# Modulation in two halves of the channels, with the first 256 tokens' products between them, at the start of a hybrid decoder block

## The chip, the cores and the metric

The kernel runs on one core of a Trainium2 chip. The time is the device time of one execution in microseconds (us). Engines: TensorE (PE in the rows; PEld its weight loads), VectorE (DVE), ScalarE (ACT), GpSimd (POOL) and SyncE (SP, which only issues transfers here). An engine works through its own instructions in their order; a semaphore lets it wait for another engine or for a transfer (DMA).

## The reference, cut to what matters

One decoder block on 2048 tokens of 1024 channels. The change touches the modulation, the normed input h and the first products with `w_in`:

```python
mod = jax.nn.silu(c) @ w_ada + b_ada            # c: (1, 1024), w_ada: (1024, 3072)
shift, scale, gate = jnp.split(mod, 3, axis=-1)
h = rms_norm(x, norm_w) * (1.0 + scale) + shift
z = h @ w_in                                     # w_in: (1024, 10240)
a, b, g_conv, q, k, v, g_attn, m_conv, m_attn = jnp.split(z, SPLIT_POINTS, axis=-1)
...
q = rope(rms_norm(q, q_norm_w), positions)       # angles = positions * inv_freq
k = rope(rms_norm(k, k_norm_w), positions)
```

Behind it come 12 attention heads of three dilations, a convolution branch, gates and the output projection, none of which the change touches.

## The kernel before

**Units and steps.** The projections of q, k and v are made head by head; one head is a unit, and unit 0 is the first. A unit has 16 steps, one for each block of 128 tokens. A step is 24 products on TensorE (line 373): for each of the eight channel blocks k the upper part of h by the upper part of the weights, the upper by the lower, and the lower by the upper (`hT_hi`, `hT_lo`, `wh_u`, `wl_u`), all added up in one bank of PSUM, `pz`. Then ScalarE squares q and k (`sq`, line 390) and copies v (`qkv`, line 400), GpSimd takes the inverse roots, and VectorE scales q and k out of the bank (`qk`, line 404) and turns them by the angles (lines 411 to 414). The banks `pz` alternate between two. A step of unit 0 also carries the preparation of the token blocks to come: a hook between two of the 24 products.

**h.** x comes in blocks of 128 tokens as rows. ScalarE squares each half (line 261), GpSimd makes the inverse root of the mean in three small operations (lines 264, 114, 115), ScalarE scales the block in two halves (line 269). TensorE turns tiles of 128 x 128 by products with `ident` (line 279, `pt_x`; four tiles a call, two channel blocks of two token blocks). Then the modulation is put on: for the first two token blocks by `h_first` (the upper part by ScalarE straight from PSUM, line 285; the same in full by VectorE, line 290; the lower part is the difference, line 292; the full one is stored to `h_d`), for later ones by `h_part` (lines 302 to 307). `hf` is its buffer, of which there are two; a buffer comes free when its store to `h_d` has ended.

**Modulation.** `c`, `b_ada` and `norm_w` are loaded as rows into `nat` and turned at once by TensorE (`pt_c`, line 147) into `cols`. silu(c) is `sc`. `w_ada` comes in eight row blocks, each in two loads of 1024 columns (shift, scale). Row blocks 1, 3 and 5 are weighted by `sc` and added up on VectorE (`sums`, lines 192 and 194); the other five and the sum go through TensorE (`ada_row`, line 201) into four banks of one row each. ScalarE copies the four rows out (`row`, line 221), 16 small turns make columns of them (`pt_ada`, line 224), and two operations of VectorE make `mod` (lines 225, 226).

**Angles.** The positions are loaded element by element into a column form (`pos_i`, line 141), the frequencies are spread over the partitions (`freq`, line 142), and VectorE makes the reduced angles in `tab` (128 x 1024) in 15 operations, between which the sums of `w_ada` stand. ScalarE takes the sines (lines 212, 213).

**What sets the order.** The order of TensorE is the program's from the units on, with x1's and x0's turns behind the modulation's fourth row block; elsewhere a scheduler places what is not pinned (`keep` pins an instruction to its place in the program). SP issues the transfers, except x0 to x3 and the first three raw weights (`raw_u`, line 343), which ScalarE's queue issues. ScalarE splits each raw weight into `wh_u` (line 349) and another engine into `wl_u` (line 352).

**Hooks of unit 0.** In step j the tiles of a later pair of token blocks are turned and modulated, two calls in an even step and two in an odd one, before product 11 and before product 19; x is squared and scaled at products 4, 9 and 12.

Of the kernel before, what the change touches and what calls it, by code (L numbers as in the profile page):

```python
# [10 lines left out]
F32 = mybir.dt.float32  # L11
# [43 lines left out]
def tile_hybrid_block(  # L55
# [67 lines left out]
    with pool("start", side="right") as st:  # L123
        keep = tc.keep_in_program_order
        nat = st.tile([4 * KC, P], F32, name="nat")
        cols = st.tile([P, 4 * KC], F32, name="cols")
        keep(nc.sync.dma_start(nat[:KC, :], c.rearrange("b (k p) -> (b k) p", p=P)))
        keep(nc.sync.dma_start(nat[KC : 3 * KC, :], b_ada[: 2 * D].rearrange("(k p) -> k p", p=P)))
        keep(nc.sync.dma_start(nat[3 * KC :, :], norm_w.rearrange("(k p) -> k p", p=P)))
        pos_i = st.tile([P, NB], I32, name="pos_i")  # L130
        freq = st.tile([P, 64], F32, name="freq")
        was = {}

        def ada_load(k):
            for half in range(2):
                wa = was[k, half] = st.tile([P, D], F32, tag="wa", name=f"wada{k}_{half}", bufs=10)
                last = keep(nc.sync.dma_start(wa, w_ada[P * k : P * k + P, D * half : D * half + D]))
            return last

        ada_load(0)  # L140
        keep(nc.sync.dma_start(pos_i, positions.rearrange("b (j p) -> p (b j)", p=P)))
        keep(nc.sync.dma_start(freq, inv_freq[None, :].to_broadcast([P, 64])))
        for k in range(1, KC):
            last_ada = ada_load(k)

        pt = bank("t", "pt_c")
        nc.tensor.transpose(pt[:, : 4 * KC], nat, ident[: 4 * KC, : 4 * KC])
        keep(nc.vector.tensor_copy(cols, pt[:, : 4 * KC]))
        th = consts.tile([P, KC], F32, name="th_c")
        with tc.high_priority():  # L150
            nc.scalar.activation(th, cols[:, :KC], AF.Tanh, scale=0.5)
        keep(nc.vector.scalar_tensor_tensor(sc, th, 1.0, cols[:, :KC], op0=ALU.add, op1=ALU.mult))
        keep(nc.vector.tensor_scalar(sc, sc, 0.5, None, op0=ALU.mult))

        pos_f = st.tile([P, NB], F32, name="pos_f")
        keep(nc.vector.tensor_copy(pos_f, pos_i))
        a = tab[:, :, 0, :]
        n = tab[:, :, 1, :]
        na = st.tile([P, NB, 64], F32, name="na")

        def angles():

            v = nc.vector

            yield v.tensor_tensor(a, pos_f[:, :, None].to_broadcast([P, NB, 64]),
                                  freq[:, None, :].to_broadcast([P, NB, 64]), op=ALU.mult)
            yield v.tensor_scalar(n, a, 1.0 / (2 * math.pi), MAGIC, op0=ALU.mult, op1=ALU.add)
            yield v.tensor_scalar(n, n, -MAGIC, None, op0=ALU.add)
            yield v.tensor_scalar(na, n, MAGIC * 2048, None, op0=ALU.add)
            yield v.tensor_scalar(na, na, -MAGIC * 2048, None, op0=ALU.add)  # L170
            yield v.tensor_sub(n, n, na)
            for part in TWO_PI:
                for t in (na, n):
                    yield v.scalar_tensor_tensor(a, t, -part, a, op0=ALU.mult, op1=ALU.add)
            yield v.tensor_scalar(a, a, -PI_LO, PI_LO, op0=ALU.max, op1=ALU.min)

        turning = angles()

        def angle_steps(count):
            for _, ins in zip(range(count), turning):  # L180
                keep(ins)


        BY_SUM = (1, 3, 5)
        acc = [bank("z", "ada0"), bank("z", "ada1"), bank("s", "ada2"), bank("s", "ada3")]
        sums = st.tile([P, 2 * D], F32, name="sums")

        def ada_sum(k):
            for half in range(2):
                part, wa = sums[:, D * half : D * half + D], was.pop((k, half))  # L190
                if k == BY_SUM[0]:
                    keep(nc.vector.tensor_scalar(part, wa, sc[:, k : k + 1], None, op0=ALU.mult))
                else:
                    keep(nc.vector.scalar_tensor_tensor(part, wa, sc[:, k : k + 1], part, op0=ALU.mult, op1=ALU.add))

        def ada_row(k):
            for half in range(2):
                wa = sums[:, D * half : D * half + D] if k is None else was.pop((k, half))
                col = ones[:, :1] if k is None else sc[:, k : k + 1]
                for i in range(2):  # L200
                    last_row = nc.tensor.matmul(acc[2 * half + i][:1, :], col, wa[:, 512 * i : 512 * i + 512],
                                                start=(k == 0), stop=(k == KC - 1))
            return last_row

        angle_steps(3)
        ada_sum(1)
        angle_steps(4)
        ada_sum(3)
        angle_steps(3)
        ada_sum(5)  # L210
# [1367 lines left out]
```

## Time and profile before

| what | us |
|---|---|
| median of three runs | 2396.71 |
| lowest, highest | 2389.79, 2397.10 |
| the profiled execution, its time | 2388.53 |
| its span, first to last instruction | 2386.7 |
| mean granted clock of TensorE | 0.996 |

A row of the timeline reads: start, length, engine, line of the kernel, operation, output <- inputs, shapes and types, number of instructions put together, and in brackets how long the engine was idle before and what ended that. Lengths of one TensorE row overlap, since products are pipelined: the distance of two starts is the pitch. In a window row the first figure is its length, then come the busy time of TensorE, its weight loads, VectorE, ScalarE and GpSimd, the granted clock of TensorE (1.00 is full speed), the share of time in which the 16 transfer engines were busy, and GB/s. A row of waits has the waiting engine and tile, what released it, the total wait, how many, and the longest.

### The profile page before, as it was taken

Reading aid. Unit: us, or ns where it says so; the run is one execution under the profiler, and the core shown is the slowest. Engines: PE = TensorE matmul, PEld = TensorE weight load, DVE = VectorE, ACT = ScalarE, POOL = GpSimd, SP = SyncE. Lnnn points to the kernel's source line nnn. Section 1 sums busy time; section 2 is a strip of 40 time slices with the busy share of each in tenths; the row PEclk is TensorE's granted clock in tenths of the full one; section 3 lists DMA queues with packets and bytes.
Section 4 is the critical chain, followed back from the end, with each engine's and each line's share of the span. In section 5 each row is a group of like instructions: output and inputs, shape, how many; then the busy total and the mean of one; then the engine's idle time right before and its main releaser. Section 6 shows DMA issues by size and latency. Waiting matters only on the chain.

```text
span 2386.7 us, 38725 instructions
## 1 busy us (share of the span) xinstructions
PE 2343.6 (98%) x12353; PEld 2088.3 (87%) x12353; DVE 1737.6 (73%) x4091; ACT 1024.4 (43%) x2850; POOL 843.8 (35%) x1003
## 2 busy tenths in 40 slices
PE   6999999999999999999999999999999999999999
PEld 2989999999999999998888888788888888878887
DVE  5865655555555777777699999979977778887654
ACT  4833433333444554456444444644444444333221
POOL 4421111111111111112577778755556730000221
PEclk9999999999999999999999999999999999999999
DMA  7633544544552222225545445744443569876552
GB/s 260 219 119 109 162 123 143 156 149 155 161 164 81 66 80 59 60 84 163 174 141 165 162 159 194 232 129 152 150 150 124 173 193 333 287 256 205 186 168 102
DMA packets 354106, 378.56 MB, mean 159 GB/s; under 512 B 29737, under 2 KB 251209, under 8 KB 353903
## 3 DMA queue, kind: packets, MB, share of 16 engines
q1 hardware_dynamic: 316414, 316.64, 42.1%
q10 hardware_dynamic: 37488, 59.46, 7.2%
q8 instruction: 98, 1.61, 0.3%
q14 instruction: 106, 0.86, 0.1%
HBM read 235.34 MB, written 140.64 MB: 158 GB/s over the span
## 4 chain that ended last, share of the span: by engine, by line
PE 89%; DVE 3%; DMA 3%; ACT 2%; POOL 1%; issue 1%; SPq 0%; ACTq 0%; DVEq 0%; POOLq 0%
PE pz L373 31%; PE paab L899 7%; PE yc L1207 5%; PE pcab L899 4%; PE pag_mc_d L899 4%; PE oa L1489 4%; PE pag_g_d L899 3%; PE ya L1207 3%; PE pag_ma_d L899 3%; PE po L502 3%; PE ps L453 3%; PE pcg_g_d L899 2%; PE oc L1489 2%; PE pbab L899 2%; PE paag L899 2%; PE pcg_mc_d L899 2%
## 5 line engine op out<-in xcount | busy, mean ns | idle before, releaser
L373 PE MATMUL pz<-wh_u,hT_lo 128*128 128x384 f32 x1536 | 537.6, 350 | 5.3 <-DVE hT_lo L292 3.8
L373 PE MATMUL pz<-wh_u,hT_hi 128*128 128x384 f32 x1536 | 518.9, 338 | 4.2 <-ACT wh_u L349 2.2
L373 PE MATMUL pz<-wl_u,hT_hi 128*128 128x384 f32 x1536 | 519.8, 338 | 0.6 <-DVE wl_u L352 0.4
L114 POOL TENSOR_SCALAR st<-st 128x2 f32<-128x2 f32 x192 | 48.3, 251 | 810.5 <-ACT sq L390 810.5
L404 DVE SCALAR_TENSOR_TENSOR qk<-pz,st,wqk 128x128 f32<-128x128 f32 x384 | 116.9, 346 | 272.3 <-POOL st L115 271.3
L373 PEld LDWEIGHTS pz<-wh_u,hT_lo 128*128 128x128 f32 x1536 | 289.6, 189 | 8.1 <-DVE hT_lo L292 4.6
L373 PEld LDWEIGHTS pz<-wh_u,hT_hi 128*128 128x128 f32 x1536 | 290.6, 189 | 6.6 <-ACT wh_u L349 2.8
L373 PEld LDWEIGHTS pz<-wl_u,hT_hi 128*128 128x128 f32 x1536 | 289.7, 189 | 1.8 <-DVE wl_u L352 1.3
L445 ACT ACTIVATE qkT<-ptq 128x256 f32<-128x256 f32 x192 | 73.9, 385 | 358.3 <-PE ptq L438 305.0
L977 DVE SCALAR_TENSOR_TENSOR ce<-us,pair_taps,ce 128x512 f32<-128x512 f32 x240 | 180.6, 753 | 6.4
L948 DVE SCALAR_TENSOR_TENSOR ce<-ut,chan,ce 128x512 f32<-128x512 f32 x240 | 178.9, 745 | 0.0
L863 POOL TENSOR_TENSOR slT<-wT,shT 128x512 fp32r<-128x512 f32 x107 | 143.9, 1346 | 79.9 <-ACT shT L862 76.7
L961 DVE SCALAR_TENSOR_TENSOR cq<-ut,chan,cq 128x512 f32<-128x512 f32 x208 | 155.3, 747 | 1.0
L862 ACT ACTIVATE shB<-wB 128x512 fp32r<-128x512 f32 x130 | 82.0, 631 | 161.3 <-PE paab L899 51.7
L390 ACT ACTIVATE sq<-pz 128x128 bf16<-128x128 f32 x384 | 105.9, 276 | 90.1 <-PE pz L373 80.8
L115 POOL TENSOR_TENSOR st<-st,mhalf 128x2 f32<-128x2 f32 x192 | 137.6, 717 | 16.0
L862 ACT ACTIVATE shT<-wT 128x512 fp32r<-128x512 f32 x110 | 69.4, 631 | 162.9 <-POOL wT L854 29.0
L863 POOL TENSOR_TENSOR slB<-wB,shB 128x512 fp32r<-128x512 f32 x85 | 111.2, 1309 | 76.9 <-ACT shB L862 76.2
L502 PE MATMUL po<-lv,pT 128*128 128x128 f32 x596 | 96.6, 273 | 0.0
L502 PEld LDWEIGHTS po<-lv,pT 128*128 128x128 f32 x596 | 91.0, 189 | 0.6 <-issue 0.5
L411 DVE TENSOR_TENSOR t<-qk,tab 128x256 f32<-128x256 f32 x192 | 82.4, 429 | 5.5
L863 POOL TENSOR_TENSOR slT<-wB,shT 128x512 fp32r<-128x512 f32 x57 | 74.9, 1321 | 27.7 <-ACT shT L862 27.7
(742 smaller groups left out, 6145.2 us busy)
## 6 DMA issues: line engine op xcount, KB each, us to landing
wB<-in_w_in_dram SPq DMA_DIRECT2D x154, 256.0 KB, 3.4
qkv_d<-qkv SPq DMA_DIRECT2D x128, 192.0 KB, 2.2
wT<-tT_d SPq DMA_DIRECT2D x88, 256.0 KB, 2.6
raw_u<-in_w_in_dram SPq DMA_DIRECT2D x93, 192.0 KB, 3.1
tT_d<-wB ACTq DMA_DIRECT2D x66, 256.0 KB, 2.2
lqk<-qkv_d SPq DMA_DIRECT2D x128, 128.0 KB, 2.2
acc_d<-osb SPq DMA_DIRECT2D x128, 65.0 KB, 1.9
part<-acc_d ACTq DMA_DIRECT2D x64, 130.0 KB, 2.2
```

The source lines that it names most:

```text
L115: nc.gpsimd.tensor_tensor(dst, scratch[:, :n], mhalf[:, :n], op=ALU.pow)
L373: nc.tensor.matmul(pz[:, :width], part(a, k, P * j, P), w[:, :width], start=(m == 0), stop=(m == 23))
L404: nc.vector.scalar_tensor_tensor(qk[:, 2 * i : 2 * i + 2].rearrange("p a b -> p (a b)"), pz[:, P * i : P * i + P], st[:, 2 + i : 3 + i], w ...
L502: nc.tensor.matmul(po[:, :P], box["pT"][:, P * i : P * i + P], vt, start=(i == 0), stop=(i == nk - 1))
L862: nc.scalar.activation(h, q[name], AF.Copy)
L863: eng.tensor_tensor(l, q[name], h.bitcast(F32), op=ALU.subtract)
L899: nc.tensor.matmul(ps, w, x, start=(m == 0 and ps.name not in first), stop=(m == 11 and not more), skip_group_check=True)
L948: stt(box["e"], e[:, 1 + j : 513 + j], chan[:, cb, 2 * j : 2 * j + 1], box["e"], op0=ALU.mult, op1=ALU.add)
L961: stt(box["o"], o[:, 2 + j : 514 + j], w, psum_o, op0=ALU.mult, op1=ALU.add)
L977: stt(dst, box["both"][:, 1 + j : 513 + j], pair_taps[:, cb, j : j + 1], box["e"], op0=ALU.mult, op1=ALU.subtract if j == 0 else ALU.add)
L1207: nc.tensor.matmul(pz, w, xx, start=(m == 0), stop=(m == len(terms) - 1))
L1489: nc.tensor.matmul(ps, y, w, start=(m == 0 and ps.name not in begun), stop=(m == 11 and not more), skip_group_check=True)
```

## The change

- **Loads.** The pool of the start is gone; its tiles now lie in the quarter tiles of h that are filled later. SP issues everything in a written order: the small rows, x0, x1, four raw weights, the first half of `w_ada` (eight pieces of 128 rows by 512 channels of shift and 512 of scale), `wqk`, x2, x3, four raw weights, the second half, x4, x5. Frequencies go on ScalarE's queue.
- **Positions** are loaded as 16 rows of 128, converted, and turned together with `c`, `b_ada` and `norm_w`.
- **Modulation by halves.** Channels 0 to 511 of shift and scale first, then 512 to 1023; all eight row blocks go through TensorE, VectorE's sums are gone. Each half has its own row copies, 8 small turns and two operations for `mod`.
- **Products between.** The upper and lower parts of the first 256 tokens for channel blocks 0 to 3 and their 24 products (both token blocks) come after the first half; blocks 4 to 7 after the second. Steps 0 and 1 of unit 0 have no products of their own any more. The turns of x2 and x3 go between the products of the second half, their modulation too.
- **Steps 2 and 3** carry the turns of token blocks 4 and 5, at products 20 and 3, 10, 17, which steps 2 and 3 carried at 11 and 19.
- **Banks.** Unit 0's steps use four banks in turn (two called z and two called s) instead of two.
- `h_first` lets ScalarE and VectorE read different banks at a time, and writes to eight buffers of its own instead of two. The squares' scrap tile has two buffers instead of one. A sine of one element loads ScalarE's table early; the table of the exponential is loaded in step 6.
- TensorE's order is the program's from the first instruction on.

```diff
-        keep(nc.sync.dma_start(pos_i, positions.rearrange("b (j p) -> p (b j)", p=P)))
-        keep(nc.sync.dma_start(freq, inv_freq[None, :].to_broadcast([P, 64])))
+    keep(nc.scalar.dma_start(freq, inv_freq[None, :].to_broadcast([P, 64])))
+    keep(nc.sync.dma_start(pos_i, positions.rearrange("b (j p) -> (b j) p", p=P)))
...
+    keep(nc.vector.tensor_copy(nat[4 * KC :, :], pos_i))
+    nc.tensor.transpose(pt[:, : 4 * KC + NB], nat, ident[: 4 * KC + NB, : 4 * KC + NB])
...
-        BY_SUM = (1, 3, 5)
-        last_mm = {k: ada_row(k) for k in (0, 2, 4, None, 6, 7)}
...
+    def ada_mm(g, acc, k):
+        for i in range(2):
+            nc.tensor.matmul(acc[i][:1, :], sc[:, k : k + 1], landed_ada(g, k)[:, i], start=(k == 0), stop=(k == KC - 1))
...
+    def first_z(kk, terms):
+        for m in terms:
+            x, w = ((hi, "h"), (hi, "l"), (lo, "h"))[m]
+            for j in range(2):
+                for k in (2 * kk, 2 * kk + 1):
+                    nc.tensor.matmul(first_pz[j][:, :384], part(x, k, P * j, P), split_w[w, k],
+                                     start=(k == 0 and m == 0), stop=(k == KC - 1 and m == 2))
...
+    x_steps = {j: squares(j, hx[j], xst[j]) for j in range(4)}
+    for i in range(4):
+        for j in range(2):
+            keep(x_steps[j][i]())
+    for k in range(4):
+        first_w(k)
+    turned = [first_turn(i, "ttoo"[i]) for i in range(4)]
+    acc = [bank("s", f"ada0{i}") for i in range(2)]
+    for k in range(KC):
+        ada_mm(0, acc, k)
+    angle_steps(20)
+    ada_row(0, acc)
+    ada_mod(0, bank("z", "pt_ada0"))
+    for kk in range(2):
+        h_first(kk)
+    first_pz = [bank("z", f"pz0_{j}") for j in range(2)]
+    for kk in range(2):
+        first_z(kk, range(3))
+    for i in range(4):
+        for j in (2, 3):
+            keep(x_steps[j][i]())
...
+    for k in range(2):
+        ada_mm(1, acc, k)
+    h_parts(2, [(kk, h_turn(2, kk)) for kk in range(2)], keep)
...
+    for k in range(2, 6):
+        ada_mm(1, acc, k)
+    pts = [(kk, h_turn(2, kk)) for kk in (2, 3)]
+    for k in range(6, KC):
+        ada_mm(1, acc, k)
+    ada_row(1, acc)
+    ada_mod(1, bank("s", "pt_ada1"))
+    for kk in (2, 3):
+        h_first(kk)
+        first_z(kk, range(3))
+    h_parts(2, pts, keep)
...
-        pz = bank("z", f"pz{n}")
-        z_tokens(pz, 384, *wts, j, hooks, u == 0 and j == 0)
+        if u == 0 and j < 2:
+            pz = first_pz[j]
+            for m in sorted(hooks):
+                for f in hooks[m]:
+                    f()
+        else:
+            pz = bank("zzss"[j % 4] if u == 0 else "z", f"pz{n}")
+            z_tokens(pz, 384, *wts, j, hooks)
...
-                    parts = (0, 1) if j % 2 == 0 else (2, 3)
-                    extra = {m: [lambda nj=nj, kk=kk: h_part(nj, kk)] for m, kk in zip((11, 19), parts)}
+                    parts = () if j < 2 else (0, 1) if j % 2 == 0 else (2, 3)
+                    hooked = {2: ((20, 4, 0),), 3: ((3, 4, 1), (10, 4, 2), (17, 4, 3))}.get(
+                        j, [(m, nj, kk) for m, kk in zip((11, 19), parts)])
```

The first place is the beginning of TensorE's order. Before, it holds the turned small rows, then the modulation:

```order
L147 MATMUL pt_c<-ident,nat 128x32
L201 MATMUL ada_171<-wada_0_127,sc 1x512
L201 MATMUL ada_172<-wada_0_127,sc 1x512
L201 MATMUL ada_173<-wada_1_129,sc 1x512
L201 MATMUL ada_174<-wada_1_129,sc 1x512
```

In the changed kernel `pt_first` are the turns of x0 and x1 (`x_151`, `x_154`), 16 in all, of which the last two are shown, and behind them the first half's products, `ada_270` the shift row and `ada_271` the scale row:

```order
L287 MATMUL pt_first_265<-ident,x_151 128x128
L287 MATMUL pt_first_265<-ident,x_154 128x128
L304 MATMUL ada_270<-first_hi_136,sc 1x512
L304 MATMUL ada_271<-first_hi_136,sc 1x512
L304 MATMUL ada_270<-first_hi_137,sc 1x512
L304 MATMUL ada_271<-first_hi_137,sc 1x512
```

The turns of x0 and x1, which stood behind the second row block of the modulation that TensorE took, now stand ahead of all of it.

The second place, on ScalarE, lies between the modulation and the first turn of token blocks 4 and 5. In the changed kernel (`x_189` is block 4, `x_192` block 5, `x_527` block 6; L252 squares, L260 scales, L494 and L504 are the evictions of steps 0 and 1, L349 the upper parts of blocks 2 and 3):

```order
L349 ACTIVATE hT_hi_206<-hf_3_500 128x2x256
L252 ACTIVATE xn_509,xst_190<-x_189 128x512 x2
L494 ACTIVATE sq_0_532,st_0_533<-pz_0_332 128x128 x2
L504 ACTIVATE qkv_0_536<-pz_0_332 128x128
L252 ACTIVATE xn_552,xst_193<-x_192 128x512
L494 ACTIVATE sq_1_560,st_1_561<-pz_1_333 128x128
L260 ACTIVATE x_189<-x_189,xst_190 128x512 x2
L252 ACTIVATE xn_552,xst_193<-x_192 128x512
L494 ACTIVATE sq_1_560,st_1_561<-pz_1_333 128x128
L504 ACTIVATE qkv_1_564<-pz_1_333 128x128
L252 ACTIVATE xn_585,xst_529<-x_527 128x512 x2
L260 ACTIVATE x_192<-x_192,xst_193 128x512 x2
```

Before, the same work stood among the upper parts of blocks 2 and 3 (`hf_0_473` and its fellows), spread over the products of steps 0 and 1 (`x_438` is block 4, `x_442` block 5):

```order
L261 ACTIVATE xn_440,xst_441<-x_438 128x512 x2
L269 ACTIVATE x_438<-x_438,xst_441 128x512
L390 ACTIVATE sq_0_504,st_0_505<-pz_0_450 128x128 x2
L400 ACTIVATE qkv_0_508<-pz_0_450 128x128
L261 ACTIVATE xn_444,xst_445<-x_442 128x512
L305 ACTIVATE hT_hi_256<-hf_0_473 128x2x256
L269 ACTIVATE x_438<-x_438,xst_441 128x512
L261 ACTIVATE xn_444,xst_445<-x_442 128x512
L305 ACTIVATE hT_hi_256<-hf_1_493 128x2x256
L269 ACTIVATE x_442<-x_442,xst_445 128x512
```

The upper parts of blocks 2 and 3 have moved ahead, and the squares and scales of blocks 4, 5 and 6 now stand with the evictions of steps 0 and 1 in one unbroken list, with block 5's scale behind block 6's squares.

More of the change, by code (lines that the diff above doesn't have):

```diff
@@ L280, in h_turn, with first_turn @@
         return pt
[L282 removed]
+    def first_turn(i, tag):
+        pt = bank(tag, f"pt_first{i}")
         for a in range(2):
[L284 to L295 removed]
@@ L317, in tile_hybrid_block @@
+    x_steps.update((j, squares(j, hx[j], xst[j])) for j in (4, 5))
+    for f in x_steps[4][:2]:
+        keep(f())
+    for t in range(1, 4):
+        quarters_of(t)
     spare = {}
@@ L604, in close_side @@
         aside.pop(tag).__exit__(None, None, None)
+    at_step(0, 6, 13, lambda: keep(nc.scalar.activation(th[:, :1], th[:, :1], AF.Exp)))
     def chan_load():
```

321 lines of the change are left out of this document (169 added, 152 removed).

## The prediction

> **What bounds the kernel now.** I read the page's first section and its chain of waits first, then the table of windows over the start, then the timeline of TensorE, and last what TensorE waited for.
>
> ```profile
> PE 2343.6 (98%) x12353; PEld 2088.3 (87%) x12353; DVE 1737.6 (73%) x4091; ACT 1024.4 (43%) x2850; POOL 843.8 (35%) x1003
> PE 89%; DVE 3%; DMA 3%; ACT 2%; POOL 1%; issue 1%; SPq 0%; ACTq 0%; DVEq 0%; POOLq 0%
> ```
>
> TensorE sets the time nearly everywhere; only the start and the first attention unit are not its own. The windows show them; each row gives the length, the busy times with their counts, the granted clock, the share of the transfer engines and GB/s.
>
> ```profile
> 0.00:45.15 45.15, 28.57 (x81) 7.22 (x81) 26.40 (x29) 20.95 (x42) 20.30 (x31) 0.96 0.84 294
> 45.15:66.00 20.85, 16.26 (x64) 14.09 (x65) 11.81 (x28) 12.85 (x30) 6.85 (x12) 0.75 0.47 158
> 66.00:106.80 40.80, 40.80 (x257) 40.10 (x257) 36.92 (x93) 34.28 (x103) 17.46 (x40) 1.00 0.69 233
> 46.70:49.90 3.20, 3.20 (x13) 3.10 (x12) 0.83 (x3) 3.18 (x6) 0.75 (x1) 0.50 0.79 257
> 58.30:63.50 5.20, 5.20 (x18) 5.10 (x19) 4.61 (x12) 3.77 (x12) 2.08 (x5) 0.50 0.32 111
> ```
>
> From 66.0 on TensorE is full for eight steps of 5.1 us, with VectorE at 90% and ScalarE at 84% beside it. Program order after about token block 4 is the same in both kernels. So the change is worth what it moves the start of step 2 (token block 2 of unit 0, at 66.0), plus what the steps behind it lose or stop losing. This is that stretch on TensorE and on the engines that release it:
>
> ```profile
> 24.58 1.97 PE L279 MATMUL pt_x<-ident,x 128*128 128x128 f32 x16
> 35.85 5.31 PE L201 MATMUL ada<-wada,sc 128*1 128x512 f32 x12
> 41.20 1.05 ACT L221 ACTIVATE row<-ada 1x512 f32<-1x512 f32 x2
> 44.09 0.40 PE L224 MATMUL pt_ada<-ident,row 1*128 1x1 f32 x4 [0.49 <-ACT row L221]
> 44.53 0.17 DVE L225 TENSOR_TENSOR mod<-pt_ada,cols 128x16 f32<-128x16 f32 x1 [1.24 <-PE pt_ada L224]
> 44.74 0.37 DVE L226 SCALAR_TENSOR_TENSOR mod<-mod,cols 128x8 f32<-128x8 f32 x1
> 45.15 3.76 ACT L285 ACTIVATE hT_hi<-pt_x,mod 128x256 fp32r<-128x256 f32 x8 [1.11 <-DVE mod L226]
> 45.76 0.44 PE L373 MATMUL pz<-wh_u,hT_hi 128*128 128x384 f32 x1 [1.27 <-ACT hT_hi L285]
> 51.01 0.99 DVE L290 TENSOR_SCALAR hf<-pt_x,mod 128x256 f32<-128x256 f32 x2 [3.48 <-DMA h_d<-hf]
> 58.60 0.52 PE L373 MATMUL pz<-wh_u,hT_hi 128*128 128x384 f32 x1
> 66.01 0.34 PE L373 MATMUL pz<-wh_u,hT_hi 128*128 128x384 f32 x1
> 66.19 0.33 PE L373 MATMUL pz<-wl_u,hT_hi 128*128 128x384 f32 x1
> ```
>
> The modulation's products end at 41.16, the first product of the block starts 4.6 later, and 48 products with 16 turned tiles take 20.25 us (45.76 to 66.01), where 48 at 0.174 and 1.97 for the turns would be 10.3. (0.174 lies between the 0.18 of the last two rows and the 0.171 of the third window: 40.80 less 64 turns of 0.12, over 192 products.) The lost 10 us are waits (VectorE's buffers come free only when a store has landed) and 8.4 us at half clock.
>
> **The change part by part.** *Start of the chain.* Before, modulation products ran first; now the 16 turns of x0 and x1 stand ahead of them in TensorE's order, so the x chain gates everything.
>
> ```profile
> 0.72 0.39 ACTq L252 DMA_DIRECT2D x<-in_x_dram  x1
> 1.55 0.31 SPq L129 DMA_DIRECT2D nat<-in_norm_w_dram  x1
> 4.51 0.63 ACT L261 ACTIVATE xn<-x 128x512 bf16<-128x512 f32 x1 [0.53 <-DMA x<-in_x_dram]
> 5.37 5.54 SPq L142 DMA_DIRECT2D freq<-in_inv_freq_dram  x1
> 11.63 1.33 ACT L269 ACTIVATE x<-x,xst 128x512 f32<-128x512 f32 x2 [2.15 <-POOL xst L115]
> 13.61 0.63 ACT L261 ACTIVATE xn<-x 128x512 bf16<-128x512 f32 x1
> 14.36 0.63 ACT L261 ACTIVATE xn<-x 128x512 bf16<-128x512 f32 x1
> 14.41 0.20 POOL L264 TENSOR_TENSOR xst<-xst 128x1 f32<-128x1 f32 x1 [2.81 <-ACT xn L261]
> 15.00 0.58 POOL L115 TENSOR_TENSOR xst<-xst,mhalf 128x1 f32<-128x1 f32 x1
> 15.92 1.04 POOL L264 TENSOR_TENSOR xst<-xst 128x1 f32<-128x1 f32 x1 [0.33 <-ACT xn L261]
> 17.80 1.26 POOL L115 TENSOR_TENSOR xst<-xst,mhalf 128x1 f32<-128x1 f32 x1
> 21.12 1.21 POOL L264 TENSOR_TENSOR xst<-xst 128x1 f32<-128x1 f32 x1 [2.06 <-ACT xn L261]
> 23.57 1.46 POOL L115 TENSOR_TENSOR xst<-xst,mhalf 128x1 f32<-128x1 f32 x1
> 48.77 0.97 PEld L279 LDWEIGHTS pt_x<-ident,x 128*128 128x128 f32 x4
> ```
>
> x0 now comes behind four small loads of SP (the last of before's three ended at 1.86, plus one more of about 0.35): issued near 2.2, and there 3.8 later (0.72 to 4.51), 6.0; x1 1.5 behind (512 KB at 350 GB/s, the first window's 294 over its share of 0.84). Squares come 0.75 apart (13.61, 14.36) and alternate between the blocks: x0's second ends near 9.0, x1's near 9.75. GpSimd's rsqrt of a block is three operations: 1.2 us while VectorE rests (14.41 to 15.58), 3.1 and 3.9 beside VectorE's wide angle operations (15.92 to 19.06, 21.12 to 25.03). Positions and frequencies are now asked for ahead of x0, so I let the angles run from about 6.5, with no weighted sums between them, over both chains: 9.0 + 3.1 = 12.1, + 3.9 = 16.0. Scaling x1's first half (half of 1.33) gives 16.7. Sixteen turns by a TensorE that has done next to nothing before cost 0.24 each (the four weight loads at 48.77, at half clock), 3.8, to 20.5. The clock may rise before they end, and the 3.8 of x0 hold a table load of ScalarE, so I take 19.5. Bounds: 15.9 if both chains take 1.2, and 20.5.
>
> *First half of the modulation.* All eight channel blocks go to TensorE now, 16 products; the trace shows each product as two passes, 0.43 apart at full clock (35.85: twelve in 5.31). 32 x 0.43 = 13.8. Still cold it loses 0 to 1.7 (a half-speed stretch of 3.4 us, as 46.5 to 49.9, is worth half of itself); I take 0.8. End: 19.5 + 0.8 + 13.8 = 34.1. The loads hide behind it: at 294 GB/s (first window) its 4.2 MB, with 1.9 MB of x and raw weights ahead, are down by about 22, while the last block is wanted at 31.
>
> *From modulation to products.* Before: 4.6 us with sixteen small turns and ScalarE's row copies split by weight copies. Now two row copies (1.05), the last small turns (0.40), 0.17 and 0.37 with gaps of 0.1: 2.3 to the modulation, and one operation of ScalarE (3.76 / 8 = 0.47) and its signal to the first product, 2.9. The 24 products of channels 0 to 511 then take 4.2 at 0.174, but not before VectorE's and GpSimd's lower parts: four 0.5 us evaluations (51.01: two in 0.99) and two subtractions put the last at 5.3, so the end is 7.4 past the modulation's end; with the clock at half for part, 8.5. I take 7.9. The eight separate buffers remove the 3.48 us wait for a store; the stores land late in SP's order, unnoticed unless their buffers are wanted.
>
> *Second half.* 13.8, and 1.97 for the 16 turns of x2 and x3 between them: 15.7. Those turns and their evaluations were in steps 0 and 1 before, on TensorE's path as well. Again 7.9. Start of step 2: 34.1 + 7.9 + 15.7 + 7.9 = 65.6, against 66.0: **-0.4**.
>
> *Steps 2 and 3.* ScalarE has the whole evictions of steps 0 and 1 and the squares and scales of x4, x5, x6 now between the second half and the first turn of x4/x5.
>
> ```profile
> 59.24 0.28 ACT L390 ACTIVATE sq<-pz 128x128 bf16<-128x128 f32 x1
> 59.51 0.27 ACT L400 ACTIVATE qkv<-pz 128x128 f32<-128x128 f32 x1
> 59.67 0.63 ACT L261 ACTIVATE xn<-x 128x512 bf16<-128x512 f32 x1
> 60.28 0.63 ACT L305 ACTIVATE hT_hi<-hf 128x512 fp32r<-128x512 f32 x1
> 60.80 0.72 ACT L269 ACTIVATE x<-x,xst 128x512 f32<-128x512 f32 x1
> ```
>
> At the pitches of these rows: x4's squares 1.2, evictions of block 0 0.8, x5's square and an eviction 1.0, x4's scales 1.2, x5's square, the rest of block 1 and x6's squares 2.4, x5's scale 0.7: 7.4. The list starts when ScalarE has the upper parts of blocks 2 and 3, 7.0 to 7.7 past the second half's end; so x5 is scaled at 14.4 to 16.0 (with 0.75 per square). TensorE wants it after 20 products of step 2, 7.9 + 3.5 = 11.4. Stall 3.0 to 4.6; I take **+3.0**. The four banks hide one thing here: step 2 need not wait for VectorE to leave block 0's bank. They do not help x5. Behind the stall VectorE gains 0.5 us per step (10%), ScalarE 0.8, so the next turns are late too: 0 to 3, I take **+1.2**.
>
> *At nothing:* positions as rows: VectorE's copy of them waits for a load, and behind it in order stand the silu of c and the angles, which the modulation wants only at 19.5. The loads of frequencies and wqk: the first held SP for 5.54 us (5.37, above); on ScalarE's queue, with nothing ahead of it, it may hold x0's first square from 6.0 to 6.3 at most. The table loads lie under the modulation's 13.8 us. Last, the waits before unit 1:
>
> ```profile
> PE pz L373 <- ACT wh_u L349: 2.2, 2, 1.3
> PE pz L373 <- DVE hT_lo L306: 1.3, 3, 0.8
> ```
>
> They stay; the order there is unchanged. Sum: -0.4 + 3.0 + 1.2 = +3.8. The profiled execution has span 2386.7 and time 2388.53, 1.8 around it, and is 8.2 below the median 2396.71; on it the forecast is 2392.3, on the median **2400.5**. Low end: 15.9 + 13.8 + 7.4 + 15.7 + 7.4 = 60.2 with no stall, -5.8, and 2 us of the waits above gone: 2389. High end: 20.5 + 1.7 + 13.8 + 2 x 7.9 + 15.7 + 3.4 (two falls of the clock, below) = 70.9, +4.9, with stalls of 4.6 and 3: +12.5, 2409, and 2 for what I cannot see.
>
> **Rivals.** *1, slower.* The clock decides. It falls in a gap: after 41.16 TensorE did 1.7 us of small turns in 4.6, and the granted clock was 0.50 in 46.7 to 49.9. The change has two gaps of 2.9 and the stall for x5. If 16 turns do not raise it (1.7 lost where I took 0.8: 0.9) and each gap lowers it (half of 3.4 is 1.7, of which 0.5 stands in the 7.9: 1.2 each), and the stall too (1.7 to 3.4, taken at 2.5), it is 3.8 + 0.9 + 1.2 + 1.2 + 2.5 = +9.6, 2406. For it: the two half-clock windows came right behind such gaps. Against: 2.9 is shorter than 4.6, with small turns inside. It is slower from 3.4 us of such loss on (7.2 less 3.8).
> The Trainium skill, "TensorE: Matmul & The Clock Gate", section "Part 4: PE-mode transpose", says that a transpose does not count as busy as a product does, so that the clock does not rise in it. By that rule all 16 turns stay at 0.24 and the modulation starts cold: the turns end at 20.5 and the whole 1.7 is lost, 1.9 more than my sum. In no window of this trace do turns stand alone.
>
> *2, faster.* GpSimd's chains run undisturbed because the angles get going late, and the four banks let steps 2 and 3 start without a stall: 3.8 - 3.6 (15.9 for 19.5) - 0.8 (warm) - 3.0 - 1.2 (no stalls) - 1.0 (7.4 twice) - 2.0 (the waits before unit 1) = -7.8, 2389. For it: the row of 1.2 us, and the angles depend on a load whose landing no row shows in its new form. Against: they have until 9.0 to be there, and all of these must go together.
>
> *3, no overlap.* The transfers pace the two halves, eight pieces of 512 KB each: at the 257 GB/s of the window at 46.7 a piece takes 2.04 us, against 1.72 of products. That adds 2.6 per half, 2405.7, and products between the halves hide nothing. For it: 84% of the transfer engines were busy in the first 45 us. Against: the lead of 9 us above.
>
> **How the numbers follow.** A difference under 0.3%, 7.2 us, cannot be told from none. Forecast 0.44 (0.38 within, 0.06 slower), rival 1 0.36 (0.33 slower, 0.03 within), rival 2 0.14 (0.10 faster, 0.04 within), rival 3 0.06 (0.03 each). Faster 0.10, same 0.48, slower 0.42. The likeliest's own range, 2389 to 2411, takes in the rivals' times and serves as the whole one.
>
> **What would show it.** Right: step 2 starts at 64 to 68; the first turn of x4 waits 2 to 5 us for ScalarE; GpSimd's chains of x0 and x1 end near 12 and 16. Wrong: a granted clock of 0.5 behind both modulations (rival 1); chains of 1.2 us and no wait in step 2 (rival 2); modulation products that wait for their loads (rival 3).

## The result and the profile after

The changed kernel takes 2402.59 us (median of 7, 2400.58 to 2405.75), the kernel before 2392.49 us in the same session: ratio 1.0040, 95% interval 1.0028 to 1.0053. That is 10.1 us more, just past the 0.3% that can be told from none. The profiled execution took 2401.77 with a span of 2398.7, 12.0 more than the span of before.

First the chain of waits of the changed kernel, which now leaves TensorE more often (85% of the span on it, 89% before):

```profile
PE 85%; DVE 5%; DMA 4%; ACT 3%; POOL 2%; issue 2%; SPq 0%; ACTq 0%; POOLq 0%; DVEq 0%
```

TensorE's waits, by stretches (0 to 65, 65 to 152, 152 to 192 us); the columns are total wait, how many, longest:

```profile
PE pt_first L287 <- DMA first_hi<-in_w_ada_dram: 8.6, 1, 8.6
...
PE pt_first L287 <- ACT x L260: 3.3, 1, 3.3
PE pz L363 <- ACT hT_hi L325: 2.1, 2, 1.1
...
PE pt_x L278 <- ACT x L260: 5.5, 3, 3.3
PE pz L471 <- ACT wh_u L449: 2.1, 1, 2.1
PE pz L471 <- DVE hT_lo L351: 1.0, 1, 1.0
PE pz L471 <- ACT hT_hi L349: 0.8, 1, 0.8
...
PE pz L471 <- ACT wh_u L449: 1.4, 1, 1.4
```

And before, from 0 to 66 and from 66 to 140 us:

```profile
PE ada L201 <- DMA wada<-in_w_ada_dram: 8.2, 2, 5.5
...
PE pz L373 <- DVE hT_lo L292: 3.8, 3, 1.5
...
PE pt_x L279 <- ACT x L269: 0.2, 1, 0.2
```

Before, TensorE stood longest at the start for the loads of `w_ada`, then for VectorE's lower parts (3.8 us), and waits for a scaled x came to 0.2. Now the waits for a scaled x (line 260) are the largest from step 2 on, 5.5 us. (The 8.6 us in the first row are put down to a load of `w_ada`, but that first turn reads x0 alone, whose scale ended just before it: the releaser is a guess there.) The timeline of TensorE, from the first turns to step 6:

```profile
16.93 3.46 PE L287 MATMUL pt_first<-ident,x 128*128 128x128 f32 x15 [3.29 <-ACT x L260]
20.32 7.92 PE L304 MATMUL ada<-first_hi,sc 128*1 128x512 f32 x16
28.07 7.03 PE L304 MATMUL ada<-first_lo,sc 128*1 128x512 f32 x16
...
37.23 1.37 PE L363 MATMUL pz<-wh_u,hT_hi 128*128 128x384 f32 x4 [1.05 <-ACT hT_hi L325]
42.01 3.59 PE L304 MATMUL ada<-first_hi,sc 128*1 128x512 f32 x8
60.26 1.36 PE L363 MATMUL pz<-wh_u,hT_hi 128*128 128x384 f32 x4 [1.05 <-ACT hT_hi L325]
64.95 0.33 PE L471 MATMUL pz<-wh_u,hT_hi 128*128 128x384 f32 x1
72.43 0.55 PE L278 MATMUL pt_x<-ident,x 128*128 128x128 f32 x3 [3.29 <-ACT x L260]
94.70 0.55 PE L278 MATMUL pt_x<-ident,x 128*128 128x128 f32 x3 [1.57 <-ACT x L260]
97.26 0.45 PE L471 MATMUL pz<-wh_u,hT_hi 128*128 128x384 f32 x1 [0.77 <-ACT hT_hi L349]
```

Step 2 starts at 64.95, 1.06 earlier than before. Then its first turn of block 4 stands for block 5's scale until 72.43, and more such waits follow. The windows of that place (length, busy times, granted clock, share of the transfer engines, GB/s):

```profile
64.95:72.40 7.45, 3.96 (x22) 3.45 (x21) 2.71 (x9) 7.36 (x27) 4.04 (x11) 1.00 0.42 145
73.35:76.76 3.41, 3.41 (x14) 3.31 (x13) 2.73 (x9) 2.54 (x9) 0.84 (x3) 0.50 0.55 198
```

ScalarE is full (7.36 of 7.45 us) while TensorE works for 3.96; right behind, TensorE runs at half clock for 3.41 us. Setting the starts of the same instructions of the two traces beside each other gives the account:

| instruction | before | after | difference |
|---|---|---|---|
| first product of step 2 | 66.01 | 64.95 | -1.1 |
| first product of step 3 | 71.10 | 73.67 | +2.6 |
| behind the half clock, step 3 | 75.23 | 79.73 | +4.5 |
| a turn in step 8 | 98.59 | 107.01 | +8.4 |
| step 14 | 134.58 | 140.68 | +6.1 |
| step 0 of unit 1 | 142.18 | 149.38 | +7.2 |
| behind a half clock there | 149.46 | 158.38 | +8.9 |

From there to the end 3 us more come. The order of instructions there is the same in both; the changed kernel's trace has half clock at 1121, 1544 and 2145 us, that of before at 1535 alone, and two such stretches of 3.41 us cost 3.4.

The largest wait behind step 2 is 1.57 us in step 6, at 94.70, and ScalarE is not its source. ScalarE itself stands for GpSimd there, one of whose operations on one column takes 2.04 us (other operations of that line take 0.2 to 0.3):

```profile
91.20 2.04 POOL L114 TENSOR_SCALAR xst<-xst 128x1 f32<-128x1 f32 x1
```

```profile
93.93 1.33 ACT L260 ACTIVATE x<-x,xst 128x512 f32<-128x512 f32 x2 [2.49 <-POOL xst L115]
```

From 91.21 to 93.17 VectorE ran four operations of two inputs with no gap between them (lines 351, 515, 516 and 351). In the trace of before the same chain of GpSimd takes 1.2 us in steps 2 to 8. Without the 1.8 us more I estimate this scale would have been there at about 92.8, before TensorE wanted it.

### The profile page after: what moved, and what is told of

It reads as the page before. It is cut to its first block, busy times and chain, and to the rows that moved or that the text cites. A ratio compares the mean times of both kernels' runs of the same rounds, so it can differ in the third digit from the quotient of the medians.

```text
span 2398.7 us, 38728 instructions
## 1 busy us (share of the span) xinstructions
PE 2348.9 (98%) x12369; PEld 2089.3 (87%) x12369; DVE 1735.5 (72%) x4088; ACT 1024.9 (43%) x2851; POOL 845.5 (35%) x1004
## 4 chain that ended last, share of the span: by engine, by line
PE 85%; DVE 5%; DMA 4%; ACT 3%; POOL 2%; issue 2%; SPq 0%; ACTq 0%; POOLq 0%; DVEq 0%
PE pz L471 29%; PE paab L990 7%; PE yc L1298 4%; PE pcab L990 4%; PE pag_mc_d L990 4%; PE pag_g_d L990 3%; PE ya L1298 3%; PE oa L1580 3%; PE pag_ma_d L990 3%; PE po L606 3%; PE ps L557 3%; PE pcg_g_d L990 2%; PE pcg_mc_d L990 2%; PE pbab L990 2%; PE ptq L542 2%
## 5 line engine op out<-in xcount | busy, mean ns | idle before, releaser
L471 PE MATMUL pz<-wh_u,hT_lo 128*128 128x384 f32 x1520 | 530.5, 349 | 1.0 <-DVE hT_lo L351 1.0
L471 PE MATMUL pz<-wh_u,hT_hi 128*128 128x384 f32 x1520 | 512.0, 337 | 4.5 <-ACT wh_u L449 3.5
L471 PE MATMUL pz<-wl_u,hT_hi 128*128 128x384 f32 x1520 | 513.0, 337 | 0.6 <-DVE wl_u L452 0.3
L494 ACT ACTIVATE sq<-pz 128x128 bf16<-128x128 f32 x384 | 105.8, 276 | 81.8 <-PE pz L471 72.7
```

Of the source, the lines that this page charges most:

```text
L471: nc.tensor.matmul(pz[:, :width], part(a, k, P * j, P), w[:, :width], start=(m == 0), stop=(m == 23))
L494: nc.scalar.activation(sq, pz[:, P * i : P * i + P], AF.Square, scale=1.0 / math.sqrt(P), accum_out=st[:, i : i + 1])
```

## The experiments

Medians are compared with runs of the kernel before on the same chip. "Both" stands for the first and the second edit together.

| kernel | us | to before | ratio, 95% interval |
|---|---|---|---|
| the change | 2402.59 | +10.1 | 1.0028 to 1.0053 |
| blocks 4, 5 early | 2398.70 | +5.1 | 1.0009 to 1.0033 |
| angles late | 2397.89 | +4.3 | 1.0004 to 1.0022 |
| both | 2394.53 | +1.0 | 0.9992 to 1.0010 |
| two banks | 2403.94 | +10.4 | 1.0023 to 1.0050 |
| both, 6 and 7 loaded early | 2393.36 | +0.1 | 0.9991 to 1.0009 |
| both, gaps filled | 2396.23 | +3.0 | 1.0002 to 1.0024 |
| lead | 2394.63 | +2.6 | 1.0006 to 1.0024 |
| lead, warm | 2393.44 | +1.4 | 0.9994 to 1.0012 |
| positions by elements | 2404.32 | +12.2 | 1.0035 to 1.0063 |
| lead, loads in order | 2387.50 | -6.7 | 0.9963 to 0.9982 |

### Blocks 4 and 5 squared and scaled early

```diff
+    x_steps.update((j, squares(j, hx[j], xst[j])) for j in (4, 5))
+    for i in range(2):
+        for j in (4, 5):
+            keep(x_steps[j][i]())
     for k in range(4, KC):
         first_w(k)
+    for i in range(2, 4):
+        for j in (4, 5):
+            keep(x_steps[j][i]())
...
-    x_steps.update((j, squares(j, hx[j], xst[j])) for j in (4, 5))
-    for f in x_steps[4][:2]:
-        keep(f())
...
-normed = {4: x_steps[4][2:], 5: x_steps[5]}
+normed = {}
```

> The changed kernel with the squares and scales of token blocks 4 and 5 moved ahead on ScalarE, into its idle stretch of 6.9 us before the second half's row copies. Theory A (these scales alone are late): the first turn of block 4 no longer waits (3.5 us gone), the half clock behind it is gone too (1.6), and the later waits for scaled blocks (1.6, 0.6) shrink; 5 to 7 us less than the changed kernel, about +3 to +5 to the kernel before; step 2 starts as before at 65 us. Theory B (ScalarE or the loads of blocks 6 on are the bound of steps 2 to 7): the wait moves to the first turns of blocks 6 and 8 and at most 2 us are won, about +8.

The wait for block 5 (3.3 us idle, 3.6 between the two turns) is gone, and 5.0 us of the 10.1. In the table of waits of this run, 70 to 165 us, those for a scaled x come to 1.6:

```profile
PE pz L475 <- ACT wh_u L453: 2.2, 2, 1.3
PE pt_x L278 <- ACT x L260: 1.6, 2, 1.0
PE pz L475 <- ACT hT_hi L349: 1.3, 3, 0.8
```

Theory A holds in its size. Its start of step 2 does not: 67.08 instead of 65, with half clock now behind both halves of the modulation (from 37.4 and from 61.3 us), in a stretch that the edit leaves alone.

### Angles held back

```diff
+    keep(nc.vector.tensor_copy(few[:, 4 * P + 65 : 4 * P + 66], xst[1][:, 1:2]))
     angle_steps(20)
```

> The changed kernel with VectorE's angles held back until GpSimd has the inverse root of block 1. Theory A (GpSimd's small operations wait for VectorE's wide ones): the two chains take about 1.2 us each instead of 3.5 and 3.8, the turns of blocks 0 and 1 start at 12 to 13.5 instead of 16.9, and everything up to step 2 comes 3.4 to 4 us earlier; +6 to the kernel before. Rival (the loads of the first half pace it): the modulation's products wait for their loads between 20 and 25 us, and less than 2 us are won, +8 to +9.

GpSimd's timeline, of the change and then of this run; the first and the last operation of the two chains:

```profile
8.82 0.75 POOL L255 TENSOR_TENSOR xst<-xst 128x1 f32<-128x1 f32 x1 [6.59 <-ACT xn L252]
10.95 1.40 POOL L115 TENSOR_TENSOR xst<-xst,mhalf 128x1 f32<-128x1 f32 x1
14.60 1.52 POOL L115 TENSOR_TENSOR xst<-xst,mhalf 128x1 f32<-128x1 f32 x1
```

```profile
9.28 0.19 POOL L255 TENSOR_TENSOR xst<-xst 128x1 f32<-128x1 f32 x1 [7.05 <-ACT xn L252]
9.88 0.58 POOL L115 TENSOR_TENSOR xst<-xst,mhalf 128x1 f32<-128x1 f32 x1
11.02 0.57 POOL L115 TENSOR_TENSOR xst<-xst,mhalf 128x1 f32<-128x1 f32 x1
```

From 8.82 to 16.12 with VectorE's operations of 1024 elements per partition beside, from 9.28 to 11.59 without: 7.3 against 2.3 us for the same six operations on one column. The turns start at 12.39, and TensorE did not wait for a load between the modulation's products; to the kernel before it is 5.8 less than the change. The rival falls. The wait for block 5 stayed, at 2.2 us instead of 3.3. In the execution that was profiled (2400.86 us, the longest of its eleven) the clock fell behind both halves, so the first half ended 4.5 us earlier than in the change (30.48) and step 2 began only 1.4 earlier (63.56).

### Both

> Both edits. If they are independent, the gains add up: 8 to 11 us less than the changed kernel, -1 to +2 to the kernel before. If ScalarE is the bound of the steps behind, the second gain is eaten by a longer wait there: +4 or more.

+1.0: the gains nearly add up (5.0 and 5.8 of 10.1, and 9.1 together). Yet the waits for a scaled x behind step 2 rose again, from 1.6 to 3.7 us: 1.04 in step 4 (blocks 6 and 7), 0.95 in step 8 and 1.67 in step 12. The last again stands behind a GpSimd operation on one column that took 2.06 us, at 120.1.

### Two banks

```diff
-pz = bank("zzss"[j % 4] if u == 0 else "z", f"pz{n}")
+pz = bank("z", f"pz{n}")
```

> The changed kernel with two banks for unit 0's steps, as before, instead of four. Theory A (the four banks hide only what the wait for block 5 costs anyway): step 2 starts 4.5 us later, when VectorE has left block 0's bank at about 69.5, its first turn then waits 0 to 1 us, and the time stays within 1.5 us of the changed kernel. Rival (the banks are worth their 4.5 us): 4 us or more above the changed kernel, +14 to the kernel before.

Within 1.4 us of the change: the banks are worth next to nothing beside the wait for block 5. Step 2 started at 70.47, after a wait of 2.9 us for VectorE to leave block 0's bank, and its turn of block 4 then waited no more.

### Blocks 6 and 7 loaded early

```diff
     turned = [first_turn(i, "ttoo"[i]) for i in range(4)]
+    ahead = {j: load_x(j) for j in (6, 7)}
...
-normed[j + 6] = load_x(j + 6)
+normed[j + 6] = ahead.pop(j + 6, None) or load_x(j + 6)
```

> Both first edits (squares and scales of blocks 4 and 5 ahead, angles held back), and the loads of token blocks 6 and 7 issued right behind those of 4 and 5 instead of in steps 0 and 1, whose hooks now run in step 2. Theory A (these two loads lost their lead when steps 0 and 1 lost their products, and the later waits for scaled blocks come from that): TensorE's waits for scaled blocks in steps 4 to 7, 3.7 us in the run with both edits, fall to 1 us or less, and the time is 2 to 3 us less, -1 to -2 to the kernel before. Rival (VectorE's and ScalarE's own load is the cause): the waits move to other blocks, less than 1 us is won.

1 us at most, to +0.1. Of the 3.7 us in the expectation only 1.04 stood in steps 4 to 7 of the run with both edits; those are gone, but 1.56 in step 6 (at 84.92) and 0.77 in step 8 (at 97.0) came. So these two loads were not what spent the lead. Step 2 began 5.8 us earlier than before; 5.2 of that held to step 6, 2.6 were left at the start of step 8 and 0.3 at the start of step 9. The wait in step 6 stands, like the one at 94.70 in the change, behind GpSimd beside the same four operations of VectorE:

```profile
81.39 2.07 POOL L114 TENSOR_SCALAR xst<-xst 128x1 f32<-128x1 f32 x1
```

```profile
84.15 1.34 ACT L260 ACTIVATE x<-x,xst 128x512 f32<-128x512 f32 x2 [2.25 <-POOL xst L115]
```

Such an operation of 1.8 to 2.2 us stands in steps 4 to 9 of every run of the change that keeps ScalarE's order there, and in steps 2 to 8 of neither the kernel before nor the runs with more lead. No run lengthens or shortens it alone, so what it cost and what the lost lead cost are not separated.

### TensorE kept busy ahead of the first turns

The two added pieces, 14 products or 25 turns whose result nothing reads, differ in one line:

```diff
+    warm = bank("z", "warm")
+    for _ in range(14):
+        nc.tensor.matmul(warm[:, :P], ident, ident, start=True, stop=True)
```

```diff
+    for _ in range(25):
+        nc.tensor.transpose(warm[:, :P], ident, ident)
```

> Both first edits, and 14 products of 128 x 128 whose result is not used, in the idle time of TensorE ahead of the turns of blocks 0 and 1. If products raise the clock, the granted clock is 1.00 before 11 us, the sixteen turns take 2.0 instead of 3.5 us, and the first half's modulation starts 1.5 us earlier, at 13.9.

> Both first edits, and 25 turns of 128 x 128 (transposes) whose result is not used, in the same place as the 14 products. If turns count as busy like products, the clock rises before 11 us here too and the sixteen turns take 2.0 us. If they do not, the added turns stay at 0.23 to 0.24 us each for their whole 6 us, the sixteen take 3.5 us as without them, and the clock rises only with the modulation's products.

The run with turns, its windows of TensorE from the added turns to the real ones, and its timeline:

```profile
6.30:9.90 3.60, 3.60 (x18) 3.60 (x18) 0.61 (x4) 2.76 (x9) 0.43 (x2) 1.00 1.09 349
10.00:11.00 1.00, 0.99 (x9) 0.75 (x7) 0.00 (x0) 0.40 (x1) 0.91 (x3) 1.00 1.01 360
```

```profile
6.28 4.72 PE L377 MATMUL warm<-ident 128*128 128x128 f32 x25
12.52 2.21 PE L287 MATMUL pt_first<-ident,x 128*128 128x128 f32 x15 [0.82 <-ACT x L260]
14.66 7.03 PE L304 MATMUL ada<-first_hi,sc 128*1 128x512 f32 x16
```

18 turns in the first 3.60 us (0.20 each), 9 in the next microsecond (0.11): the clock rose while TensorE did nothing but turns. The column of the granted clock begins with the first record of a trace, at 9.95 here, so that its 1.00 ahead of that says nothing and the pitch has to be read. Fifteen of the sixteen turns then take 2.21 us instead of 3.46. The Trainium skill, "TensorE: Matmul & The Clock Gate", section "Part 4: PE-mode transpose", has it that transposes do not bring the clock up; this run shows that they do. The products raised it too, at 8.43, but here they ended at 9.76 and TensorE idled; the clock fell again at 11.84, and nothing was won (3.31 us for the turns). One execution each took 2392.32 and 2390.65, beside 2393.24 for the kernel before.

### Gaps behind the modulation filled

```diff
+    def fill(to, count):
+        for _ in range(count):
+            nc.tensor.matmul(to[:, :384], split_w["h", 1][:, :P], split_w["h", 0], start=True, stop=True)
```

called with 2 between the two groups of four small turns and with 6 behind them, in both halves.

> Both first edits, and in each of the two gaps between a half of the modulation and its products 2 + 6 products of 128 x 384 whose result is not used. Theory (a gap in which the turns do not keep the clock up makes it fall for one window of 3.4 us, in most executions): no row of granted clock 0.50 behind either half, 1.3 us less each, in all 2 to 3 us less than both edits alone. Rival (the small turns count, and the falls come from elsewhere): the falls stay, and the time is the same or up to 0.5 us longer.

One window of 3.41 us over the gap, in the run with both edits and in this one:

```profile
29.15:32.56 3.41, 1.88 (x13) 1.35 (x13) 2.98 (x8) 2.26 (x4) 0.50 (x1) 1.00 1.05 408
```

```profile
29.57:32.98 3.41, 3.27 (x21) 2.63 (x21) 2.69 (x7) 2.29 (x4) 0.54 (x1) 1.00 1.06 410
```

Behind the first, 32.6 to 35.9 is at 0.50; behind the second nothing falls up to 1100 us, and step 2 starts at 60.09 instead of 62.20. So the mechanism that was expected is there. The time is not: +3.0, no better than both edits without it. What was won ahead of step 2 in this run was lost in the steps behind.

### One pair of blocks more of lead

```diff
     keep(nc.scalar.activation(dull, dull, AF.Sin))
+    for i in range(4):
+        for j in (2, 3):
+            keep(x_steps[j][i]())
...
-        for j in (2, 3):
+        for j in (4, 5):
             keep(x_steps[j][i]())
...
-        for j in (4, 5):
-            keep(x_steps[j][i]())
+        for j in (6, 7):
+            keep(ahead[j][i]())
```

> The run with blocks 6 and 7 loaded early, and one pair of blocks more of lead on ScalarE: blocks 2 and 3 squared and scaled under the first half's modulation, 4 and 5 behind the first half, 6 and 7 before the second half's row copies, so that steps 2 and 3 square and scale nothing. Theory A (what is won ahead of step 2 is given back in steps 4 to 8 because ScalarE's squares and scales there have lost the lead that the 20 us of steps 0 and 1 gave them): the waits for scaled blocks in steps 2 to 8, 2.3 us with blocks 6 and 7 loaded early, fall below 1 us; step 10 starts 4 us or more earlier than in the kernel before; -3 to -5 to the kernel before. Rival (a step of unit 0 takes more than 5.1 us of VectorE, GpSimd and stores whatever the lead): the lead is used up by step 8 and the time stays within 1 us of the kernel before.

> The same, with 25 turns ahead of those of blocks 0 and 1, products whose result is not used in the two gaps behind the modulation, and the table of the exponential loaded under the second half instead of in step 6. If the lead of the start comes through: the turns of blocks 0 and 1 take 2.2 us, no half clock up to step 2, which starts near 58 us, and 1 to 3 us less than the run with the lead alone. If it is given back: the same time as that run.

The second of these runs also has the 25 turns, the filled gaps, and the exponential's table loaded behind the sines. The waits for a scaled x in steps 2 to 8 fell to 1.2 us in the first run, not quite the 1 that theory A has, and to 0.2 in the second. But step 2 started at 66.5 and 66.3, and step 10 of the first run 1.9 us later than before, where theory A has it 4 earlier: x2 and x3 land late, and the copies of the modulation's rows stand behind their scales on ScalarE. The second run's own expectation did not come. Its 25 turns ended at 9.68; the clock, which had risen at 8.40, fell again from 11.81 to 15.22, the sixteen turns took 3.44 us instead of 2.2, and half clock stood from 32.3 to 39.1. The next version has 31 turns. ScalarE's timeline of the first of the two runs:

```profile
23.14 0.63 ACT L252 ACTIVATE xn<-x 128x512 bf16<-128x512 f32 x1 [7.04 <-DMA x<-in_x_dram]
...
30.03 0.72 ACT L260 ACTIVATE x<-x,xst 128x512 f32<-128x512 f32 x1 [3.68 <-POOL xst L255]
31.01 1.94 ACT L260 ACTIVATE x<-x,xst 128x512 f32<-128x512 f32 x3 [0.26 <-POOL xst L115]
32.86 1.05 ACT L308 ACTIVATE first_hi<-ada 1x512 f32<-1x512 f32 x2
```

### Positions by elements

```diff
-    keep(nc.sync.dma_start(pos_i, positions.rearrange("b (j p) -> (b j) p", p=P)))
+    keep(nc.sync.dma_start(pos_i, positions.rearrange("b (j p) -> p (b j)", p=P)))
```

> The changed kernel with the positions loaded element by element, as before, in place of the rows. Theory A (positions as rows let VectorE's angles begin at 5.4 us and so put them beside GpSimd's chains): the angles begin past 11 us, the chain of block 0 takes 1.2 us, the turns of blocks 0 and 1 start 2 to 4 us earlier; 1 to 4 us less than the changed kernel. Rival (the element loads hold up x0 and x1 in the queues): x0 lands 2 us later or more, and the turns start no earlier than in the changed kernel.

My theory fell. The angles began at 6.04 all the same, so the form of the positions had not held them back in the kernel before. There VectorE stood until 15.21 for the load of the positions, and 0.3 us more for the frequencies:

```profile
15.21 0.17 DVE L156 CAST pos_f<-pos_i 128x16 f32<-128x16 int32 x1 [8.26 <-DMA pos_i<-in_positions_dram]
```

That load was issued at 4.89 there, behind two loads of `w_ada`; here it was issued at 1.90 and the copy ran at 5.84. Its later place in the queue is the likely cause, and no run tried it alone. x0 was squared at 7.19 instead of 6.07, and the turns started at 18.85 instead of 16.93. Positions as rows are worth some 2 us at the start, which the rival foresaw in the turns (no earlier), if not in x0 (1.1 us later, not 2).

### The lead, with the loads in ScalarE's order

The version with warm turns (31 now), filled gaps and the exponential's table under the second half, and this order of loads:

```diff
-    for k in range(KC):
+    for k in range(4):
         ada_load(0, k)
-    for i, w in enumerate((q_norm_w, k_norm_w)):
-        keep(nc.sync.dma_start(wqk[:, i, :], w[None, :].to_broadcast([P, P])))
     first_x(2)
     first_x(3)
     for k in range(4, KC):
-        raw_load(k)
-    for k in range(KC):
-        ada_load(1, k)
+        ada_load(0, k)
     first_x(4)
     first_x(5)
+    for k in range(KC):
+        ada_load(1, k)
+    for k in range(4, KC):
+        raw_load(k)
+    for i, w in enumerate((q_norm_w, k_norm_w)):
+        keep(nc.sync.dma_start(wqk[:, i, :], w[None, :].to_broadcast([P, P])))
```

> The run with the lead, the added turns (31), the filled gaps and the early table, with the loads in the order in which ScalarE wants them: x2 and x3 behind the fourth piece of the first half, x4 and x5 ahead of the second half, raw weights 4 to 7 behind it. In the two runs with the lead ScalarE stood 7 to 8 us for x2 and x3 and so copied the modulation's rows 3.9 and 5.0 us late. Theory A (that wait alone ate the lead): the row copies follow the first half's products at once, step 2 starts near 58 us with the lead kept, the waits in steps 2 to 8 stay under 2 us, and the time is 4 to 7 us under the kernel before. Rival (steps 2 to 8 cannot hold 5.1 us per step for long): the lead at step 2 is given back by step 10, within 1.5 us of the kernel before.

2387.50: 6.7 us under the kernel before, and 15 to 17 under the change. TensorE's waits from 56 to 110 us, and its window over 40 us from step 2 on:

```profile
PE pt_x L280 <- ACT x L262: 0.6, 1, 0.6
```

```profile
61.65:102.00 40.35, 39.71 (x246) 38.26 (x246) 35.06 (x92) 28.33 (x90) 15.51 (x31) 1.00 0.66 218
```

Against 36.92 and 34.28 us in 40.80 before, VectorE is nearly as full (35.06) and ScalarE much less (28.33): the lead is ScalarE's. Step 2 starts 4.4 us earlier than before and at 98.6 us 3.3 of it are kept. It began at 61.65, not 58: the rows were still copied 1.9 us late, and the clock fell once behind the first half. This time it is GpSimd that ScalarE stands for, whose chains of x2 and x3 take 4.1 and 3.8 us beside VectorE's angles:

```profile
23.61 0.72 ACT L262 ACTIVATE x<-x,xst 128x512 f32<-128x512 f32 x1 [3.90 <-POOL xst L115]
27.39 1.95 ACT L262 ACTIVATE x<-x,xst 128x512 f32<-128x512 f32 x3 [3.06 <-POOL xst L115]
```

The warm turns came through (the clock was up at 8.00, the turns took 2.21 us). The rival is out. Against the run before it this version differs in the order of the loads and six turns; against the change it holds all the edits named in its expectation and in those of the runs it is built on, and what each is worth in it was not measured.

## Why the prediction came out as it did

The range held the time, and the place and the first size were right; the sum was too small, and the likeliest case (no difference that can be told) did not come. The forecast time, 2400.5, is within 2.1 us of the measured one by luck: it was built on a median of before that was 4.2 us above the one beside the result, and the difference forecast was +3.8, where +10.1 came.

- **The start of the chain**: GpSimd's two chains ended at 12.35 and 16.12 (12.1 and 16.0 forecast), the turns began at 16.93 (16.7) and took 0.23 each to their end. The first half ended at 35.03, not 34.1: the clock did not rise before the turns ended (the first record of full clock is at 22.14, the turns ended at 20.39). Angles held back and the warm turns show both causes.
- **From modulation to products**: 2.2 us, not 2.9, and the blocks of 24 ended 7.0 and 6.9 behind their half, below the bounds of 7.4 to 8.5. The last lower part was there 5.2 us behind the half, as my list had it (5.3); but only the last four products stand behind it, where I had put 12, and TensorE waited for no lower part. Step 2 began 1.1 us earlier than before, 0.4 forecast.
- **The stall in step 2**: 3.6 us, 3.0 forecast, on ScalarE's list, as the run with its early squares and scales shows. The banks hid what the forecast said they would.
- **What failed** is the step behind the stall, "the next turns are late too: 0 to 3, I take +1.2". From step 4 to step 8 the delay grew by 3.9 us (2.2 of it idle for scaled blocks, 0.8 for an upper part, the rest the work behind such waits), of which the steps to step 14 gave 2.3 back, and the way to unit 1 added 1.1. I had reckoned that ScalarE and VectorE win 0.8 and 0.5 us a step from the shares of the window 66 to 106.8; but there steps 0 and 1 had given them 20 us of lead, which the change spends. In the runs with more lead the same steps wait 0.2 to 1.2 us. What I had nowhere is GpSimd's operation of 2 us, behind which the longest of these waits stands; the runs with more lead lost it too, so how the 3.9 us divide between it and the lead stays open.
- **The clock** had no place in the likeliest sum. Up to 160 us it fell once behind the stall and once in unit 1 (half of 3.41, 1.7 us, each). Rival 1 gave 9.6 us more, and 10.1 came, but that is chance: most of it came from other parts, and the two gaps cost nothing in this execution. In six of the runs with the same gaps the clock fell behind both of them (with early blocks 4 and 5, angles late, both, two banks, warm products, positions by elements); in the change and with blocks 6 and 7 loaded early it fell behind neither.
- **Rival 2** was half made by hand with the angles held back: GpSimd's chains undisturbed won 5.8 us, and the stall, which the banks do not touch, stayed. **Rival 3** is out: the products of both halves ran without a wait for their loads.

Why unit 1's first waits rose from 2.2 to 3.5 us was not tried.

## What to carry to other kernels

A step that moves work out of a slow stage also takes away the time in which other engines ran ahead: count the lead of each helper at the point where the bound engine becomes full, not its share of busy time there. Look at which small operations of GpSimd lie beside wide ones of VectorE, at the start and wherever a scale waits for them. Here the gains ahead of step 2 were worth little until ScalarE had more lead and its loads came in its order; with both, the kernel was faster than the one before.

## What the hardware showed that was not expected

GpSimd's three operations on one column take 1.2 us alone and 3.5 to 3.8 beside VectorE's operations of 1024 elements per partition; in the steps, one of them took 2.04 us beside four shorter ones of two inputs. Turns by themselves raised the clock within 3.7 us. And the clock moves on a grid of 3.41 us that lies differently in each execution: with the same 2.2 us between the last modulation product and the first product of h, it fell behind windows with 1.88 us of work, and here, in the change itself, it did not:

```profile
35.80:39.21 3.41, 2.22 (x13) 1.88 (x14) 2.80 (x8) 2.19 (x5) 0.98 (x1) 1.00 1.05 394
```

In the run with the angles held back a window with 2.22 us of work was followed by a fall, and in the one with the warm turns a window with 2.06 was not, so these runs show no sharp border in the work of a window. The Trainium skill, "TensorE: Matmul & The Clock Gate", section "What's actually happening", calls the window free-running, of 3413 ns; the traces agree, and a gap of 2 us is therefore a matter of luck of 1.7 us in each execution.
